# A hybrid decoder layer on one core: conv gates applied behind the next weight's low part, four MLP operands fetched at another place, and the MLP's first weight sum tied behind the last residual

## The chip, the cores and the metric

The kernel runs on one core of a Trainium2 chip. The metric is the device time of one execution in microseconds (us). Three executions of the kernel before took 2448.47, 2448.91 and 2451.01 us, a median of 2448.91. TensorE (PE) multiplies, VectorE (DVE) and ScalarE (ACT) do element-wise work, GpSimd (POOL) and SyncE (SP) here mostly issue DMA transfers: SP loads weights from the inputs, POOL moves intermediate results to and from DRAM.

## What is computed

One layer over 512 tokens of width 2048, all in float32, cut to what matters here:

```python
h = rmsnorm(x, g_mix[l])
z = jnp.einsum('bsd,dc->bsc', h, w_in[l])
cb, cc, cv, q, k, v, f_logit, gate_c, gate_a = jnp.split(z, SPLIT_POINTS, axis=-1)
conv_y = cb * causal_dwconv(cc * cv, conv_w[l])
conv_branch = jnp.einsum('bsc,cd->bsd', conv_y, w_conv_out[l])
attn = forgetting_attention(q, k, v, log_f)
attn_branch = jnp.einsum('bsc,cd->bsd', attn, w_attn_out[l])
gc = jax.nn.sigmoid(gate_c + b_gate[l, :D_MODEL])
ga = jax.nn.sigmoid(gate_a + b_gate[l, D_MODEL:])
merged = gc * conv_branch + ga * attn_branch
x = x + jnp.einsum('bsd,de->bse', merged, w_mix_out[l])
h = rmsnorm(x, g_mlp[l])
u = jnp.square(jax.nn.relu(jnp.einsum('bsd,df->bsf', h, w_ff1[l])))
x = x + jnp.einsum('bsf,fd->bsd', u, w_ff2[l])
```

## The kernel before

**High and low parts.** PE multiplies operands of a short float format. Each float32 operand is therefore split into a high part, a rounded copy that ACT makes (`th`, L103), and a low part, what is left, which DVE makes by subtraction (`tl`, L104). A product takes three matmuls: high by high, high by low, low by high. A weight's low part is needed by the third matmul of its chunk (`gemm_t`, L424 to L426) or by the last third of a quarter's matmuls (`mm_rows` and `mm_cols`, L146 to L175).

**attn_out, column groups 0 to 3.** `attn_out(c)` multiplies the attention result by 512 columns of w_attn_out, in two chunks of 4 x 128 rows (`wchunk`: SP loads `raw`, then the split). Each chunk is 48 matmuls of 128x512. When a group is done, `cons_at(j)` runs for its four blocks j on DVE: `merged`, which holds the conv branch, is multiplied by the conv gate (`hg`, loaded by POOL), and the attention result times its own gate (`gt`, loaded by SP, L1006) is added (L975 or L979, through `onto`). Groups 0 and 3 have had their conv gates multiplied in earlier; groups 1 and 2 do it here. The `hg` tiles share two buffers, by the parity of j, so `hg` 2 can be loaded only when the multiplication by `hg` 0 is over. Between the chunks of group c, `all_of(c - 1)` makes the seven sums of the merged blocks that the next product needs (`M`, split as above), and `bring` fetches the held conv branch of the group two further on from `held_d` (L994).

**Products by seven.** w_mix_out, w_ff1 and w_ff2 are multiplied by a Strassen-like scheme: the weight's block of columns is cut into quarters X[0,0], X[0,1], X[1,0], X[1,1] (SP, L208), and seven products A11, A12, S1, S2, S3, S4, A22 are made of quarters or sums of quarters (L113) and of the matching operands on the other side. `Group.head` does A11 and A12, `tail2` or `tail3` the other five. After each product a list of steps (`after`) runs.

**From w_mix_out to w_ff1.** `Mix` takes the four column groups g of w_mix_out: `put` adds the residual `xr` (L116) and writes `x1_d` (L1092); `turn` transposes the result on PE, and ACT and DVE scale it and, in the last group, split it straight into the operands `A11` and `A12` of w_ff1 (L1113, L1114) or keep it in `F` (L1117). `first_of` and `sums` form the operands S1, S3, S2, S4, A22; in groups 0 to 2 `give` writes their high and low parts to `h_d` (L1133). In group 3 `begin_part` makes a tile for each w_ff1 operand and has POOL fetch what was written before: from `f_d` for A11 and A12 (L1068), from `h_d` for the other five (L1066). The last groups' share is written in directly by `Mix.out`. The first group of w_ff1, `g0`, loads X[0,0], X[1,0], X[0,1] and X[1,1] on SP and computes A11, A12, then S1, S3, S2, S4, A22; its first weight sum is X[0,1] - X[0,0] (`first_sum`, L113), which S1 multiplies, and its third is X[1,1] - X[0,1], which S3 multiplies.

**Order.** A scheduler orders each engine's instructions by priorities that follow from the program's order; an instruction in `tc.keep_in_program_order` keeps its place there against the others so marked, and `tc.issue_after(i)` puts instructions behind i. Each engine then executes its own queue in order, and a waiting instruction holds up all that is behind it on its engine; so do SP and POOL with the DMA transfers that they issue.

Of the kernel before, what the change touches and what calls it, by code (L numbers as in the profile page):

```python
# [8 lines left out]
F32 = mybir.dt.float32  # L9
# [3 lines left out]
ALU = mybir.AluOpType  # L13
# [5 lines left out]
KT = D // P  # L19
# [26 lines left out]
def tile_hybrid_block(ctx: ExitStack, tc, x, g_mix, w_in, b_f, b_gate, conv_w, w_conv_out,  # L46
                      w_attn_out, w_mix_out, g_mlp, w_ff1, w_ff2, g_final, out):
    nc = tc.nc
    x, out = x[0], out[0]
# [13 lines left out]
    def bank(i, name):  # L63
        return psum.tile([P, S], F32, tag=f"p{i}", name=name)

    def pair(i, dt, name):

        return main.tile([P, 2, D], dt, tag=f"t{i}", name=name)

    def otile(shape, name, dt=F32):  # L70
        return main.tile(shape, dt, tag="o", name=name, bufs=5)
# [9 lines left out]
    h_d = dram.tile([P, 5, 2, KT // 2 - 2, HS], F32, name="h_d")  # L81
# [20 lines left out]
    def split(src, hi, lo, one=1.0):  # L102
        a = nc.scalar.activation(out=hi, in_=src, func=AF.Copy, scale=one)  # L103
        b = nc.vector.tensor_tensor(out=lo, in0=src, in1=hi.bitcast(F32), op=ALU.subtract)  # L104
        return a, b

    def split_in_order(*how):

        for i in split(*how):
            tc.keep_in_program_order(i)  # L110

    def sub(out, a, b):
        return nc.vector.tensor_tensor(out=out, in0=a, in1=b, op=ALU.subtract)  # L113

    def add(out, a, b):
        nc.vector.tensor_tensor(out=out, in0=a, in1=b, op=ALU.add)  # L116

    def parts(shape, at=0):

        q, w = shape[1:]  # L120
        return tuple(main.tile([P, WBUF], F32R, tag=tag, name=tag, bufs=2)[:, at:at + q * w]
                     .rearrange("p (q c) -> p q c", q=q) for tag in ("th", "tl"))
# [67 lines left out]
    class Group:  # L190
# [128 lines left out]
            self.plus(s2, d)  # L319
            self.put(1, 0, s2)  # L320

        def first_sum(self):

            self.pinned = True
            X = self.X
            X[0, 1] = self.load(0, 1)
            tc.keep_in_program_order(sub(X[0, 0], X[0, 1], X[0, 0]))

        def tail2(self):

# [69 lines left out]
    def wchunk(view, k0, c0, slot):  # L400

        raw = main.tile([P, 4, S], F32, tag=f"x{slot}", name="raw")
        nc.sync.dma_start(out=raw, in_=view[k0 * P:(k0 + 4) * P, c0:c0 + S].rearrange("(q p) c -> p q c", p=P))
        hi, lo = parts([P, 4, S])
        split(raw, hi, lo)
        return hi, lo

    turns, cycle = [0], [0, 3, 2]

    def slot():  # L410
# [49 lines left out]
    class Quarters:  # L460
# [20 lines left out]
        def put(self, n, src, ts=slice(0, HS), one=1.0):  # L481
            split(src[:, :, ts], self.ST[n][:, 0, :, ts], self.ST[n][:, 1, :, ts], one)
# [326 lines left out]
    n = 0  # L809
# [162 lines left out]
    def onto(c, j, g, op):  # L972
        if c in whole_of:
            o = whole_of[c][:, :, j % 2, j // 2, :]
            nc.vector.tensor_tensor(out=o, in0=o, in1=g.rearrange("p (h s) -> p h s", h=2), op=op)  # L975
        else:
            for h in range(2):
                o = merged[c][h][:, j % 2, j // 2, :]
                nc.vector.tensor_tensor(out=o, in0=o, in1=g[:, h * HS:(h + 1) * HS], op=op)  # L979
# [17 lines left out]
    def attn_out(c, banks, last=False, **how):  # L997

        def cons_at(j, ps):
            if c not in GATED:  # L1000
                hg = pm.tile([P, S], F32, tag=("xr", "s1")[j % 2], name="hg")
                nc.gpsimd.dma_start(out=hg, in_=g_d[0, 4 * c + j])
                onto(c, j, hg, ALU.mult)
            g = otile([P, S], "gt")
            nc.sync.dma_start(out=g, in_=g_d[1, 4 * c + j])
            nc.vector.tensor_tensor(out=g, in0=ps, in1=g, op=ALU.mult)  # L1006
            onto(c, j, g, ALU.add)
            if last and j == 2:
                M.place(3, [(n, 3) for n in ("A11", "A12", "S1", "S2")])
                M.place(2, [("S4", 3), ("S3", 3), ("A22", 3), ("A22", 2)])  # L1010
                for e in range(2):
                    nc.gpsimd.dma_start(out=M.at["A22", 2][e].bitcast(F32), in_=m22[e].bitcast(F32))
                quads3.update(M.quads(3, merged[3]))
                quads3["A11"]()
            if last and j == 3:
                quads3["A12"]()

        gemm_t(w_attn_out, CT, c * S, aact, banks, cons_at, **how)
# [31 lines left out]
    n = turns[0] + 1  # L1050
# [4 lines left out]
    Q2 = {}  # L1055
# [4 lines left out]
    SPLIT = ("S1", "S3", "S2", "S4", "A22")  # L1060

    def begin_part(n, k):

        Q2[n] = pair(k, F32R, n).rearrange("p e (q s) -> p e q s", q=KT // 2)
        if n in SPLIT:
            nc.gpsimd.dma_start(out=Q2[n][:, :, :KT // 2 - 2].bitcast(F32), in_=h_d[:, SPLIT.index(n)])  # L1066
        else:
            nc.gpsimd.dma_start(out=Q2[n][:, 1, :KT // 2 - 2].bitcast(F32), in_=f_d[:, int(n == "A12")])  # L1068

    def split_part(n):  # L1070
        lo = Q2[n][:, 1, :KT // 2 - 2]
        split_in_order(lo.bitcast(F32), Q2[n][:, 0, :KT // 2 - 2], lo)

    class Mix:
# [13 lines left out]
        def put(self, i, j, v):  # L1088
            g = self.g
            c = g * S + j * HS  # L1090
            add(v, v, self.x.pop((i, j)))
            nc.gpsimd.dma_start(out=x1_d[2 * i:2 * i + 2, :, c:c + HS].rearrange("t p c -> p t c"), in_=v)  # L1092
            waiting.append(lambda: self.turn(i, j, v))
            if (i, j) == (0, 0):
                self.rows(1, 1, otile([P, 2, HS], "xr"))
                self.rows(0, 1, pm.tile([P, 2, HS], F32, tag="xr", name="xr"))
# [83 lines left out]
    for g in range(4):  # L1180
        mix = mixes[g] = Mix(g)
        after = Steps()
        if g == 0:
            for n, n2 in zip(("A11", "A12", "S1", "S3", "S2"), ("S1", "S3", "S2", "S4", "A22")):
                after.add(n, quads3[n2])
        if g == 3:
            after.add("S1", mix.fourth, lambda: begin_part("A12", 4))
        late = g == 1
        for n in ("A12", "S3") if late else ("A11", "S1"):
            after.add(n, turn_waiting)  # L1190
        after.add("A22", turn_first)
        if before:
            after.add("A12" if late else "A11", before.first_of, before.sums)
            for n, part in (("A12", "S1"), ("S1", "S3"), ("S2", "A22")):
                after.add(n, lambda before=before, part=part: before.give(part))
        if g < 3:
            after.add("S2", mix.fourth)
        else:
            after.add("A12", lambda: begin_part("A11", 0))
            after.add("S2", lambda: begin_part("S1", 1), lambda: begin_part("S3", 3))  # L1200
            after.add("S4", lambda: split_part("A11"))
            after.add("S3", lambda: begin_part("S2", 5))
            after.add("A22", lambda: begin_part("S4", 6), lambda: begin_part("A22", 2), lambda: split_part("A12"))
        group = groups[g]
        group.after = after
        if g == 0:
            after.add("A11", group.first_sum)
        if g == 3:
            group.mid["A22"] = turn_first
        group.head(True, between=groups[1].first if g == 0 else lambda: None)  # L1210
        (group.tail2 if g < 3 else group.tail3)()
        before = mix
    def factors(common, r):

        ms = const.tile([P, NT], F32, name="ms")
        nc.vector.tensor_reduce(out=ms, in_=ss2, axis=AX.X, op=ALU.add)
        nc.gpsimd.tensor_tensor(out=r, in0=ms, in1=mhalf.to_broadcast([P, NT]), op=ALU.pow)
        ones = const.tile([P, P], F32, name="ones")
        nc.vector.memset(ones, 1.0 / S)
        pt = bank(6, "mean")  # L1220
        nc.tensor.matmul(pt[:, :NT], ones, ms, start=True, stop=True)
        mean, back = (const.tile([P, 1], F32, name=n) for n in ("mean", "back"))
        nc.vector.tensor_reduce(out=mean, in_=pt[:, :NT], axis=AX.X, op=ALU.add)
        nc.gpsimd.tensor_tensor(out=common, in0=mean, in1=mhalf, op=ALU.pow)
        nc.vector.reciprocal(out=back, in_=common)
        nc.vector.tensor_scalar(out=r, in0=r, scalar1=back, scalar2=None, op0=ALU.mult)
        nc.vector.tensor_tensor(out=r, in0=r, in1=r, op=ALU.mult)
# [49 lines left out]
    def ff1(g, banks):  # L1277
# [3 lines left out]
    common, turned = const.tile([P, 1], F32, name="common"), const.tile([P, NT], F32, name="turned")  # L1281

    g0 = ff1(0, ((5,), (0,), (1,), (7,)))
    g0.after = Steps(A11=[g0.first_sum, turn_waiting, mix.first_of],
                     A12=[lambda: mix.out("S1", mix.s1), mix.sums, lambda: factors(common, turned)])
    g0.head(True)
    for n in SPLIT[1:]:
# [248 lines left out]
```

## Time and profile before

| | us |
|---|---|
| median of three executions | 2448.91 |
| profiled execution, its own time | 2452.95 |
| its span in the profile | 2451.2 |
| PE busy | 2410.0 |
| DVE busy | 2042.6 |
| ACT busy | 1203.0 |
| POOL busy | 280.0 |

The profile shows one execution. In a timeline row stand the start in us from the span's beginning, the duration, the engine, the line of the kernel, the operation, the tile written and the tiles read, and in brackets the idle time of the engine before the instruction with what ended it. Some starts overlap the end of the row before, because the instructions of an engine are pipelined; a chain's length is therefore read from start to start. Rows of stretches give for each engine the busy time, then PE's granted clock (1.00 is full), the share of the DMA engines that was busy and the bytes moved. In the queue rows stand packets, MB and the time that the packets took as a share of 16 engines.

### The profile page before, as it was taken

The page shows a single profiled execution, that of the slowest core. Times are in us where ns is not written, and L with a number is a line of the kernel's source. Part 1 is how long each engine was busy: PE and PEld are TensorE (multiplying, and loading weights), DVE is VectorE, ACT ScalarE, POOL GpSimd, SP SyncE. Part 2 cuts the span into 40 slices and gives each one's busy share as a digit, 9 for nine tenths or more (in the row PEclk, how much of TensorE's full clock was granted, in tenths as well). Part 3 has the DMA queues.
Part 4 walks back from the last instruction along what each step waited for, and adds up shares of the span by engine and source line. Part 5 has one row for each costly group of instructions (what it writes and reads, how often), then busy time and mean ns, then how long its engine had stood idle before and what let it go on. Part 6 is the DMA issues. An engine that isn't in the chain of part 4 may idle for free.

```text
span 2451.2 us, 41539 instructions
## 1 busy us (share of the span) xinstructions
PE 2410.0 (98%) x17800; PEld 2266.2 (92%) x17800; DVE 2042.6 (83%) x1725; ACT 1203.0 (49%) x1233; POOL 280.0 (11%) x450
## 2 busy tenths in 40 slices
PE   8999999999999999999999999999999999999998
PEld 8999899999999999899899999999997888888886
DVE  6987777788888778898889898898978888889898
ACT  6443433345455444355656666666655333333334
POOL 0100000111121111112300000000011001100000
PEclk9999999999999999999999999999999999999999
DMA  7564444444656655757855655656587576655663
GB/s 250 181 187 147 154 135 143 142 154 167 216 170 214 213 189 189 237 162 252 306 183 186 228 189 199 236 182 228 194 304 271 168 248 227 236 190 183 245 223 103
DMA packets 287628, 491.97 MB, mean 201 GB/s; under 512 B 11900, under 2 KB 199412, under 8 KB 287060
## 3 DMA queue, kind: packets, MB, share of 16 engines
q1 hardware_dynamic: 237072, 283.20, 36.3%
q0 software_dynamic: 49504, 205.02, 22.5%
q8 instruction: 139, 2.28, 0.4%
q10 hardware_dynamic: 868, 1.10, 0.1%
q14 instruction: 45, 0.37, 0.0%
HBM read 378.65 MB, written 110.10 MB: 199 GB/s over the span
## 4 chain that ended last, share of the span: by engine, by line
PE 86%; DVE 5%; issue 4%; DMA 3%; POOL 1%; ACT 1%; DVEq 0%; SPq 0%; POOLq 0%; ACTq 0%
PE a L157 6%; PE a L153 6%; PE a L155 6%; PE a L175 5%; PE a L173 5%; PE a L172 5%; PE d L157 5%; PE d L153 5%; PE d L155 5%; PE c L153 4%; PE c L155 4%; PE c L157 4%; PE d L175 3%; PE d L173 3%; PE d L172 3%
## 5 line engine op out<-in xcount | busy, mean ns | idle before, releaser
L103 ACT ACTIVATE th<-x 128x2048 fp32r<-128x2048 f32 (+1 forms) x280 | 536.9, 1918 | 501.1 <-DVE x L113 169.3
L104 DVE TENSOR_TENSOR tl<-x,th 128x2048 fp32r<-128x2048 f32 (+1 forms) x280 | 639.5, 2289 | 166.3 <-ACT th L103 151.3
L113 DVE TENSOR_TENSOR x<-x,x 128x2048 f32<-128x2048 f32 (+1 forms) x160 | 366.3, 2289 | 28.5 <-DMA x<-in_w_in_dram 17.4
L103 ACT ACTIVATE th<-y 128x2048 fp32r<-128x2048 f32 (+1 forms) x109 | 185.4, 1702 | 273.8 <-PE a L173 138.8
L104 DVE TENSOR_TENSOR tl<-y,th 128x2048 fp32r<-128x2048 f32 (+1 forms) x109 | 219.1, 2014 | 29.1 <-ACT th L103 28.6
L172 PE MATMUL a<-th,us 128*128 128x512 f32 x512 | 199.4, 389 | 2.2 <-ACT th L103 2.2
L173 PE MATMUL a<-th,us 128*128 128x512 f32 x512 | 199.5, 390 | 0.0
L153 PE MATMUL c<-S,th 128*128 128x256 f32 x848 | 196.7, 278 | 0.0
L155 PE MATMUL c<-S,th 128*128 128x256 f32 x848 | 196.3, 277 | 0.0
L153 PE MATMUL a<-S,th 128*128 128x256 f32 x784 | 182.3, 278 | 0.0
L155 PE MATMUL a<-S,th 128*128 128x256 f32 x784 | 180.9, 277 | 0.0
L153 PEld LDWEIGHTS c<-S,th 128*128 128x128 f32 x848 | 159.4, 188 | 0.3
L155 PEld LDWEIGHTS c<-S,th 128*128 128x128 f32 x848 | 159.4, 188 | 0.0
L155 PEld LDWEIGHTS a<-S,th 128*128 128x128 f32 x784 | 147.4, 188 | 0.0
L153 PEld LDWEIGHTS a<-S,th 128*128 128x128 f32 x784 | 147.3, 188 | 0.0
L175 PE MATMUL a<-tl,us 128*128 128x512 f32 x512 | 137.0, 390 | 0.6 <-DVE tl L104 0.6
L155 PE MATMUL a<-A,th 128*128 128x256 f32 x544 | 126.0, 278 | 2.2 <-DVE A L1114 2.2
L153 PE MATMUL d<-S,th 128*128 128x256 f32 x544 | 128.0, 280 | 0.0
L155 PE MATMUL b<-A,th 128*128 128x256 f32 x544 | 126.4, 278 | 1.3 <-DVE A L104 1.3
L155 PE MATMUL d<-S,th 128*128 128x256 f32 x544 | 127.4, 279 | 0.0
L153 PE MATMUL b<-A,th 128*128 128x256 f32 x544 | 126.4, 278 | 0.0
L153 PE MATMUL a<-A,th 128*128 128x256 f32 x544 | 126.1, 278 | 0.0
(378 smaller groups left out, 6076.5 us busy)
## 6 DMA issues: line engine op xcount, KB each, us to landing
x<-in_w_in_dram SPq DMA_DIRECT2D x86, 1024.0 KB, 5.9
x<-in_w_ff_dram SPq DMA_DIRECT2D x64, 1024.0 KB, 8.5
y<-in_w_ff_dram SPq DMA_DIRECT2D x64, 1024.0 KB, 7.9
us<-s_d POOLq DMA_DIRECT2D x48, 1024.0 KB, 9.5
s_d<-rh POOLq DMA_DIRECT2D x32, 896.0 KB, 5.5
s_d<-r POOLq DMA_DIRECT2D x32, 896.0 KB, 5.9
x<-in_w_mix_out_dram SPq DMA_DIRECT2D x17, 1024.0 KB, 6.9
g_d<-o POOLq DMA_DIRECT2D x32, 256.0 KB, 2.8
```

Source lines behind the costliest of these rows:

```text
L103: a = nc.scalar.activation(out=hi, in_=src, func=AF.Copy, scale=one)
L104: b = nc.vector.tensor_tensor(out=lo, in0=src, in1=hi.bitcast(F32), op=ALU.subtract)
L113: return nc.vector.tensor_tensor(out=out, in0=a, in1=b, op=ALU.subtract)
L153: nc.tensor.matmul(o, hi[:, q, js], Sh, start=first and q == 0 and j == 0, stop=False, skip_group_check=True)
L155: nc.tensor.matmul(o, hi[:, q, js], Sl, start=False, stop=False, skip_group_check=True)
L157: nc.tensor.matmul(o, lo[:, q, js], Sh, start=False, stop=q == nq - 1, skip_group_check=True)
L172: nc.tensor.matmul(o, Sh, hi[:, q, :], start=begin and q == 0, stop=False, skip_group_check=True)
L173: nc.tensor.matmul(o, Sl, hi[:, q, :], start=False, stop=False, skip_group_check=True)
L175: nc.tensor.matmul(o, Sh, lo[:, q, :], start=False, stop=q == nq - 1, skip_group_check=True)
```

## The change

The conv gate multiplications of groups 1 and 2 are put behind the latest low part that `wchunk` has made. `first_sum` of g0 is no longer kept in program order, and is put behind the last residual sum of the last group (`mix.added`), after the steps that turn what is waiting. The fetches of S2, S4 and A22 come in a step of g0's A11, that of S3 after S3 in group 3 of w_mix_out instead of after S2, and the fetches from `h_d` keep their program order. `Mix.put` makes its sum by the same instruction as before, with its handle kept.

```diff
-        def first_sum(self):
+        def first_sum(self, pinned=True):
...
-            tc.keep_in_program_order(sub(X[0, 0], X[0, 1], X[0, 0]))
+            one = sub(X[0, 0], X[0, 1], X[0, 0])
+            if pinned:
+                tc.keep_in_program_order(one)
...
-        split(raw, hi, lo)
+        chunk_low.append(split(raw, hi, lo)[1])
         return hi, lo
+    chunk_low = []
...
                 nc.gpsimd.dma_start(out=hg, in_=g_d[0, 4 * c + j])
-                onto(c, j, hg, ALU.mult)
+                with tc.issue_after(chunk_low[-1].ins):
+                    onto(c, j, hg, ALU.mult)
...
         if n in SPLIT:
-            nc.gpsimd.dma_start(out=Q2[n][:, :, :KT // 2 - 2].bitcast(F32), in_=h_d[:, SPLIT.index(n)])
+            tc.keep_in_program_order(
+                nc.gpsimd.dma_start(out=Q2[n][:, :, :KT // 2 - 2].bitcast(F32), in_=h_d[:, SPLIT.index(n)]))
...
-            add(v, v, self.x.pop((i, j)))
+            self.added = nc.vector.tensor_tensor(out=v, in0=v, in1=self.x.pop((i, j)), op=ALU.add)
...
             after.add("A12", lambda: begin_part("A11", 0))
-            after.add("S2", lambda: begin_part("S1", 1), lambda: begin_part("S3", 3))
+            after.add("S2", lambda: begin_part("S1", 1))
             after.add("S4", lambda: split_part("A11"))
-            after.add("S3", lambda: begin_part("S2", 5))
-            after.add("A22", lambda: begin_part("S4", 6), lambda: begin_part("A22", 2), lambda: split_part("A12"))
+            after.add("S3", lambda: begin_part("S3", 3))
+            after.add("A22", lambda: split_part("A12"))
...
+    def begin_rest():
+        for n, k in (("S2", 5), ("S4", 6), ("A22", 2)):
+            begin_part(n, k)
+
+    def first_sum_after(ins):
+        with tc.issue_after(ins.ins):
+            g0.first_sum(pinned=False)
...
-    g0.after = Steps(A11=[g0.first_sum, turn_waiting, mix.first_of],
+    g0.after = Steps(A11=[turn_waiting, begin_rest, lambda: first_sum_after(mix.added), mix.first_of],
```

## The prediction

> **What bounds the kernel now.** I began with the page's header and busy row.
>
> ```profile
> span 2451.2 us, 41539 instructions
> PE 2410.0 (98%) x17800; PEld 2266.2 (92%) x17800; DVE 2042.6 (83%) x1725; ACT 1203.0 (49%) x1233; POOL 280.0 (11%) x450
> ```
>
> TensorE (PE) is busy 2410.0 of 2451.2 us, so the change matters only where it shortens, lengthens or makes a stall of PE, or alters PE's clock. PE's timeline, which prints the idle time before an instruction and its releaser, shows the stalls in the two places that the diff touches. The first row is the start of attn_out's second chunk of column group 2 (I call the chunks c2k0, c2k4, c3k0, c3k4); its third matmul, the first to read the low part tl, is the second row.
>
> ```profile
> 1000.57 0.39 PE L424 MATMUL pt<-act,th 128*128 128x512 f32 x1
> 1002.96 0.50 PE L426 MATMUL pt<-act,tl 128*128 128x512 f32 x1 [1.78 <-DVE tl L104]
> ...
> 1015.60 0.39 PE L426 MATMUL pt<-act,tl 128*128 128x512 f32 x1
> ...
> 1211.25 0.39 PE L155 MATMUL a<-A,th 128*128 128x256 f32 x1 [2.15 <-DVE A L1114]
> 1217.40 0.38 PE L155 MATMUL b<-A,th 128*128 128x256 f32 x1 [1.30 <-DVE A L104]
> 1230.95 0.36 PE L146 MATMUL d<-S,th 128*128 128x192 f32 x1 [2.06 <-ACT th L103]
> ```
>
> Four stalls, 1.78 + 2.15 + 1.30 + 2.06 = 7.29 us. Cutting the span into stretches shows that they cost more than their own length.
>
> ```profile
> 1000.00:1004.00 4.00, 2.22 (x10) 1.55 (x9) 4.00 (x5) 1.15 (x2) 0.14 (x1) 0.97 0.26 90
> 1004.00:1008.00 4.00, 4.00 (x12) 3.13 (x12) 4.00 (x8) 2.14 (x4) 0.58 (x1) 0.60 0.90 208
> ...
> 1212.00:1216.00 4.00, 4.00 (x21) 3.80 (x20) 3.52 (x4) 3.48 (x10) 2.16 (x3) 0.58 1.01 402
> ...
> 1224.00:1236.00 12.00, 9.94 (x72) 9.73 (x71) 9.89 (x13) 4.26 (x5) 0.56 (x1) 0.86 0.29 116
> ```
>
> The columns are PE, PEld, DVE, ACT and POOL busy, then the granted clock, the share of the DMA engines and GB/s. Behind the 1.78 us stall the clock is 0.60: lost are 4 x 0.03 + 4 x 0.40 = 1.7 us. Behind the stalls of 2.15 and 2.06 it is 0.58 and 0.86 (4 x 0.42 = 1.7 and 12 x 0.14 = 1.7 us); the 1.30 us one is followed by none of its own. I call this a half-clock window, and put its threshold between 1.30 and 1.78 us.
>
> [...]
>
> **The change, part one: the conv gates of column group 2.** The four multiplications by hg move behind the low part of c2k4. In DVE's rows two of them stand ahead of that low part today:
>
> ```profile
> 997.03 0.69 DVE L975 TENSOR_TENSOR merged<-merged,hg 128x512 f32<-128x512 f32 x1 [0.42 <-DMA hg<-g_d]
> 997.64 0.68 DVE L104 TENSOR_TENSOR M<-merged,M 128x512 fp32r<-128x512 f32 x1
> 998.61 0.69 DVE L975 TENSOR_TENSOR merged<-merged,hg 128x512 f32<-128x512 f32 x1 [0.29 <-DMA hg<-g_d]
> 999.22 0.69 DVE L1006 TENSOR_TENSOR gt<-pt,gt 128x512 f32<-128x512 f32 x1
> ...
> 1000.62 2.28 DVE L104 TENSOR_TENSOR tl<-raw,th 128x2048 fp32r<-128x2048 f32 x1
> ...
> 1008.24 0.69 DVE L975 TENSOR_TENSOR merged<-merged,hg 128x512 f32<-128x512 f32 x1
> ...
> 1010.23 2.29 DVE L104 TENSOR_TENSOR tl<-raw,th 128x2048 fp32r<-128x2048 f32 x1
> ```
>
> They take 0.42 + 0.61 + 0.29 + 0.61 = 1.93 us (starts to starts). Comparing the built orders, the sum s now stands ahead of tl too, another 0.6, and the M low part still has to wait some 0.4 for its high part on ACT. So tl starts 1.93 - 0.6 - 0.4 = 0.9 us sooner. PE's third matmul is due two pitches of 0.22 after 1000.57, at 1001.0, and came at 1002.96; the wait goes from 1.9 to 1.0 us. At 1.0 the half-clock window goes too. Won: 0.9 + 1.7 = 2.6 us.
>
> What is late next is the low part of c3k0. In the built order DVE does hg 0, 1 and 2 ahead of it, hg 3 after it. hg 0 and hg 2 share one buffer, so POOL can fetch hg 2 only when multiplication 0 is done. Today's first hg of the later pair starts 1008.24 - 1000.62 = 7.6 us behind c2k4's tl; with tl at 999.7 and s taken out of the stretch that is 999.7 + 7.6 - 0.6 = 1006.7 for multiplication 0, and its end at 1007.4 releases the fetch, at about 1007.5. What a fetch costs there has two near rows: the same hg loads at 994 to 1000 and the merged loads that POOL issues from 1007.42, min/median/max to landing:
>
> ```profile
> DMA to landing us min/median/max: 2.8/2.9/3.1
> ```
>
> ```profile
> L994 POOL DMA_DIRECT2D merged<-held_d x4: 712/723/729, 1007.4 to 1011.5; - x4
> ...
> DMA to landing us min/median/max: 4.9/5.9/6.0
> ```
>
> The first four flew while DVE had PE fed and the DMA engines had gaps; the second at a DMA share of 0.90 (the 1004 to 1008 row). Two of the merged loads now stand right ahead of hg 2 in POOL's queue, so I take 5.0, nearer to 5.9. hg 2 lands at 1012.5, its multiplication (0.6) and tl (2.2) end at 1015.3. PE wants it at 1015.60 - 2.6 = 1013.0: a new stall of 2.3 us, and, above the threshold, a half-clock window of 1.7. Part one: -2.6 + 4.0 = +1.4 us. With 2.9 it is landing 1010.4, end 1013.2, stall 0.2: -2.4. With 5.9: stall 3.2 and 1.7: +2.3. The four gt loads move ahead of the next w_mix load on SP; that load's data is first read behind both chunks of group 3, 96 matmuls or 21 us, so I count nothing. If c3k4's tl, with under 1 us to spare, is late as well, this is inside the upper end.
>
> **Part two: the last residual and the first weight sum of ff1.** DVE's queue today:
>
> ```profile
> 1208.51 2.29 DVE L113 TENSOR_TENSOR x<-x,x 128x2048 f32<-128x2048 f32 x1 [6.33 <-DMA x<-in_w_ff_dram]
> 1210.72 0.48 DVE L1114 SCALAR_TENSOR_TENSOR A<-ptr,cols,A 128x256 fp32r<-128x256 f32 x1
> ...
> 1212.84 2.28 DVE L104 TENSOR_TENSOR tl<-x,th 128x2048 fp32r<-128x2048 f32 x1
> 1215.59 1.76 DVE L104 TENSOR_TENSOR A<-A 128x1536 fp32r<-128x1536 f32 x1 [0.48 <-ACT A L103]
> 1217.79 2.29 DVE L104 TENSOR_TENSOR tl<-x,th 128x2048 fp32r<-128x2048 f32 x1 [0.44 <-ACT th L103]
> ...
> 1226.61 2.29 DVE L113 TENSOR_TENSOR x<-x,x 128x2048 f32<-128x2048 f32 x1
> ...
> 1228.99 1.91 ACT L103 ACTIVATE th<-x 128x2048 fp32r<-128x2048 f32 x1 [2.44 <-DVE one L1432]
> ```
>
> The sub at 1208.51 waits 6.33 us for quarter (0,1) of w_ff1, and two L1114 and two L116 queue behind it, 1210.72 to 1212.84 = 2.12 us. They now run in that idle time. The PE wait at 1211.25 for L1114 goes, though PE then only comes sooner to A12, whose third matmul waits for A's low part (1215.59), which still stands behind the sub. Five S1 matmuls moved ahead of that third matmul wait for the same sub through th, no later than A's low part ends. From sub to the third sum (1226.61) the chain loses 2.12, the waits 0.48 and 0.44 (ACT is no longer held up by L1114), and the reciprocal and turned pair, about 0.29, which now follow it: 3.33 us. If (0,1) lands as today, A12 goes on at 1217.40 - 2.12 - 0.48 = 1214.8, and S3, which waits for th of the third sum, starts at 1230.95 - 3.33 = 1227.6. Part two would be -3.3.
>
> **Part three: what POOL fetches when.** It decides whether (0,1) lands as today.
>
> ```profile
> 1195.12 0.71 POOL L1066 DMA_DIRECT2D S<-h_d  x1 [9.57 <-DMA h_d<-s]
> 1195.83 0.57 POOL L1133 DMA_DIRECT2D h_d<-staged  x1
> ...
> 1208.01 0.71 POOL L1066 DMA_DIRECT2D S<-h_d  x1 [10.01 <-DMA h_d<-f]
> ```
>
> POOL sits 9.57 us in front of the S1 load with four h_d writes behind it, then 10.01 us in front of S3. In the built order the four writes come ahead of S1, the x1_d writes between S1 and S3; S2, S4 and A22 behind both. So the queue has no such pauses, and S3's 1.5 MB go out some 5 to 9 us sooner. What a pause is worth to SP's weight loads shows in the queues' bytes from 1193.5 to 1198.5 and from 1198.5 to 1208.5 (q1 is SP's, q0 POOL's):
>
> ```profile
> q1 hardware_dynamic: 1636, 1.66, 102.0%
> q0 software_dynamic: 31, 0.13, 6.3%
> ```
>
> ```profile
> q0 software_dynamic: 592, 2.62, 65.0%
> q1 hardware_dynamic: 1214, 1.21, 35.3%
> ```
>
> Alone SP's queue moves 1.66 / 5 = 0.33 MB per us, beside POOL's 1.21 / 10 = 0.12. If the whole pause fills with writes, SP is 5 x (0.33 - 0.12) = 1.06 MB behind at 1198.5. Paid back at 0.33 that delays (0,1) by 3.2 us, at 0.12 by 8.7; if POOL's data still start as late as today, by 0. I take 3.2, as POOL must still wait for its own writes before S1 and S3 and for the last residual before S2, and in each such gap SP has the engines. Then part two and three together are 3.2 - 3.33 = -0.1 us (0: -3.3; 8.7: +5.4). PE is not the limit there: A12 goes on at 1214.8 + 3.2 = 1218.0 and has as much work to S3 as today (1217.40 to 1230.95 less the stall of 2.06 is 11.5), done at 1229.5 against S3's 1230.8. I leave both half-clock windows of this stretch as they are, since PE still idles for long before A12's third matmul; the one at S3 is open (a stall of 1.3), which is worth 1.7 down.
>
> [...]
>
> **Sum.** Profiled execution 2452.95 us (span 2451.2, 1.75 outside) + 1.4 - 0.1 = 2454.2. The profiled execution lies 4.04 above the median 2448.91; I take the same off: 2450.2 us.
>
> **Rivals.** (a) Both loads come in time: hg 2 lands in 2.9 and (0,1) as today. For it: the hg rows, and the waits of POOL for its own writes. Against it: a DMA share of 0.9 and 1.0 in both places. 2452.95 - 2.4 - 3.3 - 4.04 = 2443.2. (b) Slower: SP's queue starves. POOL's writes, S1, S3 and then S2, S4, A22 follow each other without a pause, (0,1) lands 8.7 late, and DVE, with tl of A12, A's low part and all of S1 and S3 behind the sub, stands still. From a delay of 3.3 it costs more than part two wins. With hg 2 at 5.9: 2452.95 + 2.3 + 5.4 - 4.04 = 2456.6. For it: both transfers share 16 busy engines. Against it: total bytes do not grow, and the x1_d write of the last residual holds S2 back. (c) hg 2 lands fast, the sub late by 3.2: 2452.95 - 2.4 - 0.1 - 4.04 = 2446.4. Its counterpart, hg 2 late and (0,1) in time, gives 2447.0, by 1.4 - 3.3.
>
> **How the numbers follow.** About 0.2%, 4.9 us, is what a measurement of this kernel can tell from no change: faster is below 2444.0, slower above 2453.8. The forecast, gains given back at hg 2 and at (0,1), has 0.33, (a) 0.25, (b) 0.29, (c) with its counterpart 0.13. (a) ends faster, at 2443.2; a lost window at S3 in (c) adds 0.02: faster 0.27. (b) is slower, mostly, and the forecast's tail of a longer hg wait reaches there: slower 0.30. The rest, 0.43, is within the bound. The range goes from just under (a) to 2456.0, which takes in the smaller delays of (b), and leaves out about 0.2. The likeliest case alone is 2447 to 2453.
>
> **What would show it.** Right: the stall at c2k4 is near 1.0 without a slow clock behind it; a new one at c3k0's tl, with DVE waiting for hg. The L1114 row sits ahead of the sub, and the sub's releaser is still the w_ff1 load, some 3 us later than 1208.5; POOL's S3 load goes out before 1204; S3's first matmul is within 1.5 us of 1230.95, reckoned from the same start. Wrong: hg is never waited for; or the sub starts by 1209 or after 1214; or the third sum waits for (1,1); or a wait past 1240.

## The result, and the profile after

Over 20 executions of each on the same chips the changed kernel took 2455.88 us (2451.27 to 2462.66) and the kernel before 2450.60 us (2447.39 to 2454.15). The ratio is 1.0022, 95% interval 1.0016 to 1.0028: slower by 5.4 us, 3.9 to 6.9. The prediction was 2450.2 us in a range from just under 2443.2 to 2456.0, with "within 0.2%" as the likeliest. The time is inside the range, 0.1 us from its upper end; the change of 0.22% is just past the bound on the slow side, and its interval (0.16 to 0.28%) reaches to both sides of that bound.

The profiled execution of the changed kernel took 2454.11 us (span 2452.4), 1.8 us under its median, while the one of before, 2452.95, lies 2.4 over the median of its 20. The difference of the two profiles, 1.2 us, is therefore less than the change costs; they show where time goes, and the sizes are taken from the experiments. Header and busy row of the page after:

```profile
span 2452.4 us, 41546 instructions
## 1 busy us (share of the span) xinstructions
PE 2407.9 (98%) x17800; PEld 2263.3 (92%) x17800; DVE 2042.3 (83%) x1725; ACT 1203.3 (49%) x1233; POOL 281.6 (11%) x450
```

PE's work is the same, so the place to look is its stalls. PE's timeline after, the rows with idle time that answer to those of before, and the new ones (the line numbers have moved by 3 to 6):

```profile
1002.52 0.50 PE L429 MATMUL pt<-act,tl 128*128 128x512 f32 x1 [1.23 <-DVE tl L104]
1014.80 0.50 PE L429 MATMUL pt<-act,tl 128*128 128x512 f32 x1 [1.11 <-DVE tl L104]
...
1061.63 0.95 PE L175 MATMUL d<-tl,M 128*128 128x256 f32 x6 [0.52 <-DVE tl L104]
1068.49 0.97 PE L175 MATMUL a<-tl,M 128*128 128x256 f32 x6 [0.94 <-DVE tl L104]
...
1216.02 0.36 PE L146 MATMUL b<-A,th 128*128 128x192 f32 x1 [3.63 <-ACT A L103]
1218.74 0.58 PE L153 MATMUL c<-S,th 128*128 128x256 f32 x1 [2.23 <-ACT th L103]
1220.61 0.58 PE L155 MATMUL b<-A,th 128*128 128x256 f32 x1 [0.43 <-DVE A L104]
1234.22 0.36 PE L146 MATMUL d<-S,th 128*128 128x192 f32 x1 [1.36 <-ACT th L103]
1240.88 0.39 PE L153 MATMUL a<-S,th 128*128 128x256 f32 x1 [0.81 <-ACT th L103]
```

At c2k4 the stall is shorter, 1.23 instead of 1.78 us. For that there are three others: at c3k0 (1014.80), and two at the first quarters of w_mix_out (1061.63 and 1068.49), where PE did not wait before. At the MLP the stalls of 2.15, 1.30 and 2.06 us have become 3.63, 2.23, 0.43, 1.36 and 0.81. Just ahead of that, near 1180 us, the changed kernel waits less: 0.35 us in all against 0.94 and 0.85 before. The clock, from the cut into stretches:

```profile
1000.00:1004.00 4.00, 2.77 (x12) 1.99 (x11) 4.00 (x5) 0.93 (x2) 0.00 (x0) 1.00 0.37 95
1004.00:1008.00 4.00, 4.00 (x19) 3.33 (x18) 4.00 (x8) 2.55 (x4) 1.44 (x2) 1.00 0.95 252
...
1216.00:1224.00 8.00, 5.32 (x24) 4.83 (x25) 8.00 (x8) 4.91 (x10) 3.01 (x1) 0.57 1.02 414
1224.00:1236.00 12.00, 10.64 (x92) 10.43 (x91) 9.65 (x16) 5.30 (x7) 0.56 (x1) 1.00 0.21 84
```

The half-clock window behind c2k4 is gone (1.00 instead of 0.60 from 1004 to 1008), and so is the one behind S3. At the MLP one long stretch at 0.57 has taken the place of the two, and costs as much as they did together: 8 x 0.43 = 3.4 us.

DVE's timeline after tells what the new stalls wait for:

```profile
1008.41 0.68 DVE L978 TENSOR_TENSOR merged<-merged,hg 128x512 f32<-128x512 f32 x1
1011.86 0.69 DVE L978 TENSOR_TENSOR merged<-merged,hg 128x512 f32<-128x512 f32 x1 [2.77 <-DMA hg<-g_d]
1012.47 2.28 DVE L104 TENSOR_TENSOR tl<-raw,th 128x2048 fp32r<-128x2048 f32 x1
...
1206.83 0.69 DVE L1096 TENSOR_TENSOR o<-o,xr 128x512 f32<-128x512 f32 x1
1214.40 2.29 DVE L113 TENSOR_TENSOR x<-x,x 128x2048 f32<-128x2048 f32 x1 [6.88 <-DMA x<-in_w_ff_dram]
1216.61 2.28 DVE L104 TENSOR_TENSOR tl<-x,th 128x2048 fp32r<-128x2048 f32 x1
1218.81 1.75 DVE L104 TENSOR_TENSOR A<-A 128x1536 fp32r<-128x1536 f32 x1
```

DVE waits 2.77 us for hg 2 right ahead of c3k0's low part, and the first weight sum of ff1 starts at 1214.40 instead of 1208.51, still for want of quarter (0,1).

ACT's timeline after shows that quarter (1,0), which the prediction did not reckon with, lands late too:

```profile
1210.44 1.92 ACT L103 ACTIVATE th<-x 128x2048 fp32r<-128x2048 f32 x1 [5.57 <-DMA x<-in_w_ff_dram]
...
1214.48 1.49 ACT L103 ACTIVATE A<-A 128x1536 fp32r<-128x1536 f32 x1
```

ACT waits 5.57 us for (1,0), and so makes A's high part late, for which PE waits 3.63 us. PE then has only half a us of work until its next stall, at 1218.74, which the first weight sum's high part ends. So it is the late (0,1) that ends PE's waiting. (In e7 below, where (1,0) came sooner, the first of these stalls is 0.79 us and the second 4.46.)

POOL's and SP's bytes from 1204.5 to 1209.5, ahead of that landing, are in the queue rows after:

```profile
q0 software_dynamic: 324, 1.72, 84.2%
q1 hardware_dynamic: 322, 0.33, 18.6%
```

Columns are packets, MB and the share of the engines. In that stretch of before POOL's queue ran nearly dry: it moved 0.77 MB, of which 0.09 after 1207.0, and SP's moved 0.81.

```profile
q1 hardware_dynamic: 803, 0.81, 45.5%
q0 software_dynamic: 240, 0.77, 42.2%
```

### The profile page after: what moved, and what is told of

It is laid out like the page before. It is cut to its first block, busy times and chain, and to the rows that moved or that the text cites. A ratio compares the mean times of both kernels' runs of the same rounds, so it can differ in the third digit from the quotient of the medians.

```text
span 2452.4 us, 41546 instructions
## 1 busy us (share of the span) xinstructions
PE 2407.9 (98%) x17800; PEld 2263.3 (92%) x17800; DVE 2042.3 (83%) x1725; ACT 1203.3 (49%) x1233; POOL 281.6 (11%) x450
## 4 chain that ended last, share of the span: by engine, by line
PE 83%; DVE 7%; issue 4%; DMA 4%; ACT 1%; POOL 1%; SPq 0%; DVEq 0%; POOLq 0%; ACTq 0%
PE a L157 6%; PE a L153 6%; PE a L155 6%; PE a L175 5%; PE a L173 5%; PE a L172 5%; PE d L153 5%; PE d L155 5%; PE d L157 5%; PE c L153 4%; PE c L155 4%; PE c L157 4%; DVE tl L104 3%; PE d L175 3%; PE d L173 3%
```

## The experiments

The theory was: (A) the fetch of hg 2 costs PE twice, at once and again where DVE's lateness surfaces; (C) the sum behind the residual wins, and POOL's new order takes more than that back, because the weight quarters land late. The main rivals: all of the loss lies at the MLP, the moved waits cost nothing, or the transfers are hidden. Each kernel was timed 11 or 12 times, against 29 or 33 executions of the kernel before on the same chip. The us are the ratio less one, times 2451.

| kernel | ratio to before | 95% interval | us |
|---|---|---|---|
| changed kernel | 1.0022 | 1.0016 to 1.0028 | +5.4 |
| e1 part one | 1.0005 | 0.9997 to 1.0014 | +1.2 |
| e2 part one, own buffers | 0.9999 | 0.9991 to 1.0008 | -0.2 |
| e3 part two | 0.9989 | 0.9980 to 0.9998 | -2.7 |
| e4 part three | 1.0022 | 1.0013 to 1.0031 | +5.4 |
| e5 parts one and two | 0.9997 | 0.9988 to 1.0006 | -0.7 |
| e6 e2 and part two | 0.9983 | 0.9974 to 0.9992 | -4.2 |
| e7 changed, own buffers | 1.0007 | 0.9998 to 1.0016 | +1.7 |
| e8 parts two and three, S3 late | 0.9985 | 0.9976 to 0.9994 | -3.7 |
| e9 changed, S3 late | 0.9995 | 0.9987 to 1.0004 | -1.2 |
| e10 part three, S3 late | 1.0004 | 0.9996 to 1.0012 | +1.0 |
| e11 e6 and e8 together | 0.9984 | 0.9976 to 0.9993 | -3.9 |

**e1: part one alone.**

```diff
-        split(raw, hi, lo)
+        chunk_low.append(split(raw, hi, lo)[1])
...
-                onto(c, j, hg, ALU.mult)
+                with tc.issue_after(chunk_low[-1].ins):
+                    onto(c, j, hg, ALU.mult)
```

> Part one alone: the conv gates of group 2 behind the low part of c2k4; first sum and fetches as before. Theory A (the fetch of hg 2 costs twice): DVE waits 2 to 3 us for hg 2, PE stalls some 1.5 us at the third matmul of c3k0, and DVE, which has no idle time from there to the first quarters of w_mix_out, stays about 2 us late, so that PE stalls again there (0.8 and 1.2 us in the changed kernel, none before). Net of the 0.5 us won at c2k4: slower than before by 2 to 4 us, and nothing different from before after 1180 us but a shift. Rival B (all of the loss lies at the MLP): within 1 us of before, or faster by the 0.5 us and a half-clock window of 1.7.

The time does not tell +1.2 from nothing (-0.7 to +3.4), and the 2 to 4 us expected are at most partly there. The trace does show the expected wait and stalls. DVE's and PE's timelines of e1:

```profile
1011.65 0.69 DVE L976 TENSOR_TENSOR merged<-merged,hg 128x512 f32<-128x512 f32 x1 [3.14 <-DMA hg<-g_d]
```

```profile
1061.44 0.97 PE L175 MATMUL d<-tl,M 128*128 128x256 f32 x6 [0.48 <-DVE tl L104]
1068.29 0.97 PE L175 MATMUL a<-tl,M 128*128 128x256 f32 x6 [0.93 <-DVE tl L104]
```

The same wait and the same two late stalls as in the changed kernel, without its parts two and three. The wait and the first of the stalls belong to part one; whether the second does, e2 and e3 tell.

**e2: as e1, with other buffers for hg 2 and 3 of group 2.**

```diff
-                hg = pm.tile([P, S], F32, tag=("xr", "s1")[j % 2], name="hg")
+                hg = pm.tile([P, S], F32, tag=("xr", "s1")[j % 2], name="hg") if j < 2 or c == 1 else otile([P, S], "hg")
```

> As e1, but hg 2 and 3 of group 2 get buffers of the pool of gt tiles, so that their fetch no longer waits for the multiplications by hg 0 and 1. Theory A: DVE no longer waits for hg 2, the stall at c3k0 and the two at w_mix_out vanish, the shorter stall at c2k4 stays: 2 to 4 us under e1, 0.5 to 2 us under before. If the wait is not the cause (rival: four multiplications in front of c3k0's low part are too many by themselves, 4 x 0.6 = 2.4 us), the stalls at w_mix_out stay, and e2 lies within 1 us of e1.

DVE's timeline of e2 at the same place:

```profile
1007.70 0.68 DVE L104 TENSOR_TENSOR M<-merged,M 128x512 fp32r<-128x512 f32 x1
1008.30 1.88 DVE L976 TENSOR_TENSOR merged<-merged,hg 128x512 f32<-128x512 f32 x3
1010.11 2.28 DVE L104 TENSOR_TENSOR tl<-raw,th 128x2048 fp32r<-128x2048 f32 x1
```

The multiplications by hg follow each other and the low part starts 2.4 us sooner than in the changed kernel (1010.11 against 1012.47). The stall at c3k0 and the first of the two at w_mix_out are gone. The second is not. PE's timelines of e2 and then of e3, whose gates are those of before:

```profile
1065.66 0.97 PE L175 MATMUL a<-tl,M 128*128 128x256 f32 x6 [0.89 <-DVE tl L104]
```

```profile
1066.71 0.96 PE L175 MATMUL a<-tl,M 128*128 128x256 f32 x6 [0.46 <-DVE tl L104]
```

So theory A is wrong on this stall: 0.89 us stay without the wait for hg 2, against 0.93 with it, and half of it is there without part one. Against e1 the gain is only 1.4 us where 2 to 4 were expected, and within the intervals; three pairs with and without these buffers (e2 and e1, e6 and e5, e7 and the changed kernel) give 1.4, 3.5 and 3.7 us, and together they show that the wait costs time.

**e3: part two alone** (`first_sum_after(mix.added)` behind `turn_waiting`; POOL's order is that of before).

```diff
-    g0.after = Steps(A11=[g0.first_sum, turn_waiting, mix.first_of],
+    g0.after = Steps(A11=[turn_waiting, lambda: first_sum_after(mix.added), mix.first_of],
```

> Part two alone: the first weight sum of ff1 behind the last residual; gates and fetches as before. Theory C: quarter (0,1) lands as before, the sub starts at about 1208.5 us, and the two L1114 and two residual sums run in the wait ahead of it. S3's first matmul starts some 3 us sooner than 1230.95; faster than before by 2 to 3.5 us. Rival D (PE's wait is only moved): the longer single wait before A12's third matmul costs as much as the two it replaces, same as before within 1 us.

DVE's and PE's timelines of e3:

```profile
1205.02 0.48 DVE L1116 SCALAR_TENSOR_TENSOR A<-ptr,cols,A 128x256 fp32r<-128x256 f32 x1 [0.54 <-ACT A L1115]
...
1209.06 2.29 DVE L113 TENSOR_TENSOR x<-x,x 128x2048 f32<-128x2048 f32 x1 [1.42 <-DMA x<-in_w_ff_dram]
```

```profile
1213.81 0.39 PE L153 MATMUL c<-S,th 128*128 128x256 f32 x1 [1.06 <-ACT th L103]
1215.28 0.39 PE L155 MATMUL b<-A,th 128*128 128x256 f32 x1 [0.61 <-DVE A L104]
...
1228.29 0.35 PE L146 MATMUL d<-S,th 128*128 128x192 f32 x1 [2.10 <-ACT th L103]
```

The sub waits for the load as before, but the four instructions that it held up have run. S3 starts 2.7 us sooner. That speaks against rival D, that the wait is only moved, and so does the time, -2.7 us (-4.9 to -0.5), though the end of its interval touches that rival's 1 us. In this execution no half-clock window followed any of these stalls (the clock is 1.00 from 1208 to 1240), where before shows two.

**e4: part three alone.**

```diff
-            nc.gpsimd.dma_start(out=Q2[n][:, :, :KT // 2 - 2].bitcast(F32), in_=h_d[:, SPLIT.index(n)])
+            tc.keep_in_program_order(
+                nc.gpsimd.dma_start(out=Q2[n][:, :, :KT // 2 - 2].bitcast(F32), in_=h_d[:, SPLIT.index(n)]))
...
-            after.add("S2", lambda: begin_part("S1", 1), lambda: begin_part("S3", 3))
+            after.add("S2", lambda: begin_part("S1", 1))
...
-            after.add("S3", lambda: begin_part("S2", 5))
+            after.add("S3", lambda: begin_part("S3", 3))
...
-    g0.after = Steps(A11=[g0.first_sum, turn_waiting, mix.first_of],
+    g0.after = Steps(A11=[g0.first_sum, turn_waiting, begin_rest, mix.first_of],
```

> Part three alone: POOL's fetch order; gates and first sum as before. Theory C: POOL's writes and the S3 fetch now move beside SP's weight loads, quarter (1,0) lands some 10 us and (0,1) 4 to 6 us later than before, the L1114 behind the sub are late by as much, and PE with them: slower than before by 4 to 6 us. Rival D (bytes are the same, the transfers are hidden): the sub starts within 1 us of 1208.5 and the time is that of before within 1 us.

It costs as much as the whole change. DVE's timeline of e4, and PE's:

```profile
1211.96 2.29 DVE L113 TENSOR_TENSOR x<-x,x 128x2048 f32<-128x2048 f32 x1 [10.30 <-DMA x<-in_w_ff_dram]
```

```profile
1214.70 0.58 PE L155 MATMUL a<-A,th 128*128 128x256 f32 x1 [5.93 <-DVE A L1115]
```

The wait of 6.33 us for quarter (0,1) has grown to 10.30, and the stall that was 2.15 us to 5.93. That the transfers are hidden is ruled out.

**e5 and e6: parts one and two, and the same with e2's buffers.**

> The change without its part three: gates and first sum as changed, POOL's fetches and writes as before. Theory C (part three is the whole loss): e1 and e3 add, +1 and -3 us: 1 to 3 us faster than before and 6 to 8 us faster than the changed kernel; quarter (0,1) lands within 1.5 us of 1209. Rival (the first sum behind the residual costs when hg makes DVE late): not faster than before.

> e2 and e3 together: gates with buffers of their own, first sum behind the last residual, fetches as before. Theory A and C: no wait for hg, sub at about 1209; the fastest so far, 3 to 5 us under before and 1 to 2 us under e5. If hg's wait costs nothing in the end, e6 equals e5.

e5 lies 6.1 us under the changed kernel by the ratios, as expected; the 1 to 3 us under before are not shown (-0.7, -2.9 to +1.5). In its trace the sub starts at 1207.53. e6 is 4.2 us under before (2.0 to 6.4), as expected, and beats both kernels; it lies 3.5 us under e5, more than the 1 to 2 expected.

**e7: the changed kernel with e2's buffers, nothing else.**

> The changed kernel with buffers of their own for hg 2 and 3 and nothing else altered. Theory A: the wait for hg and the three stalls behind it vanish, the late weight quarters stay: 1 to 3 us faster than the changed kernel, still slower than before by 2 to 4 us. Rival B: same as the changed kernel.

+1.7 instead of +5.4: the two intervals meet only at their edges, at 1.0016. By the ratios the fetch of hg 2 costs the changed kernel 3.7 us, more than the 1 to 3 expected and more than e1 shows for it; from the two intervals I estimate 1 to 6. The traces show less: from c2k4's third matmul to SP's first load of w_ff1 the changed kernel takes 181.7 us (1002.52 to 1184.24) and e7 180.1 (1001.90 to 1181.95), 1.7 us apart. The stall at w_mix_out that Theory A expected to vanish with the others, the second, stands here too, with 0.91 us.

**e8: parts two and three with the S3 fetch late.**

```diff
-            after.add("S3", lambda: begin_part("S3", 3))
...
-        for n, k in (("S2", 5), ("S4", 6), ("A22", 2)):
+        for n, k in (("S3", 3), ("S2", 5), ("S4", 6), ("A22", 2)):
```

> Parts two and three without the gates, and with the S3 fetch put behind the last x1_d write, next to S2, S4 and A22; the four h_d writes stay ahead of the S1 fetch. Theory E (the 1.5 MB of S3 beside the weight quarters are what delays them): quarter (0,1) lands within 1.5 us of 1209, and the time is within 1 us of e3, some 3 us under before. Rival F (the writes in POOL's former pause are it): (0,1) lands at 1212 or later as in the changed kernel, and the time is 2 to 6 us over before.

POOL's timeline, DVE's and ACT's of e8:

```profile
1193.16 1.14 POOL L1136 DMA_DIRECT2D h_d<-f  x2 [0.72 <-DVE f L104]
1196.02 0.72 POOL L1069 DMA_DIRECT2D S<-h_d  x1 [1.71 <-DMA h_d<-s]
...
1210.88 2.15 POOL L1069 DMA_DIRECT2D S<-h_d  x3 [1.62 <-PE a L155]
```

```profile
1210.30 2.29 DVE L113 TENSOR_TENSOR x<-x,x 128x2048 f32<-128x2048 f32 x1 [2.06 <-DMA x<-in_w_ff_dram]
```

```profile
1207.67 1.92 ACT L103 ACTIVATE th<-x 128x2048 fp32r<-128x2048 f32 x1 [2.10 <-DMA x<-in_w_ff_dram]
```

The four writes still go ahead of the S1 fetch, and ACT now waits for quarter (1,0) until 1207.67. But the sub starts at 1210.30, not 1214.40, or 25.4 us instead of 30.2 behind SP's first load of w_ff1 (1184.86 and 1184.24), and the loss has become a gain of 3.7 us. So it is the early S3 fetch that makes (0,1) late in a way that costs; what the writes cost, e10 tells. With S3 late the scheduler also puts the third sum's low part ahead of the turned pair, which may be a part of the gain.

**e9 to e11.** e9 is the changed kernel with e8's edit, e10 part three with it, e11 e6 and e8 together.

> The changed kernel with one fetch moved: S3 behind the last x1_d write, ahead of S2 (which also lets the scheduler put the third sum's low part ahead of the turned pair). Theory E: quarter (0,1) lands 3 to 5 us sooner than in the changed kernel, counted from the issue of (0,0); 4 to 7 us faster than the changed kernel, within 1.5 us of e5. Rival F (the writes ahead of S1): same as the changed kernel within 1 us.

> Part three alone with S3 behind the last x1_d write; gates and first sum as before. Tells what the four writes ahead of S1 cost by themselves, as (1,0) is late and (0,1) is not. Theory E: (1,0) lands near 1208 as in e4 and e8 but PE does not wait for it; same as before within 1.5 us, 4 to 6 us under e4. Rival F: the late (1,0) holds up th of A12 and with it A's low part, 3 us or more over before.

> e6 and e8 together: buffers of their own for hg 2 and 3, first sum behind the last residual, the writes ahead of S1, S3 behind the last x1_d write. If the causes named are all there is, as fast as e6 and e8, 3 to 5 us under before; the order of the four writes gives nothing more.

e9: one fetch moved lets the sub start 25.5 us behind SP's first load of w_ff1 (1186.69 to 1212.19) instead of 30.2. It takes 6.6 us off the changed kernel, and the time is then that of e5, within the intervals. e10: the writes ahead of S1, with S3 late, cost 1.0 us, which the measurement does not tell from nothing, and 4.4 us less than e4. e11 is as fast as e6, so the order of the writes and of S3 gives nothing further. The order of the four writes was not tried alone with S3 early.

## Why the prediction came out as it did

The point was that the gains are given back at two new waits, at hg 2 and at quarter (0,1). Both are where it said. The time came out 5.7 us above the forecast: 1.7 of it is the base (below), and some 4 the balance of gains and losses, forecast +1.3 and measured +5.4. That the time lies in the range is owed to the width that was taken for rival (b), and it is a matter of 0.1 us.

Of the signs that the prediction named, these came: the shorter stall at c2k4 without a slow clock, the new one at c3k0 with DVE waiting for hg, the L1114 pair (now L1119, at 1203.87 and 1204.90) ahead of the sub, the sub still waiting for the w_ff1 load, the S3 fetch before 1204 (at 1199.92). Two did not, and both are of part three. The sub, due some 3 us later than 1208.5, started at 1214.40, past the 1214 that was named as a sign of being wrong (1213.6 with the 0.8 us taken off by which the whole program was late there). S3's first matmul, due within 1.5 us of 1230.95, came at 1234.22, 2.5 us late with the same 0.8 taken off.

- **Part one, won at c2k4:** forecast 0.9 us and a half-clock window, 1.7. The low part did come 0.9 us sooner, counted from DVE's wait for hg just ahead (992.51 to 1000.62 before, 992.99 to 1000.18 after); as that wait itself ended 0.48 later, the stall fell by 0.55 only (1.78 to 1.23). The window went in this execution, but a part of its 1.7 us seems to come back: of the five kernels with the gates of before, the two with a slow clock behind c2k4 (before, e8) do not wait at 1066 us, and the three without (e3, e4, e10) wait 0.46, 0.50 and 0.46 there.
- **Part one, the wait for hg 2:** forecast landing at 1012.5 after 5.0 us; the multiplication started at 1011.86, as the fetch went ahead at 1008.2 and took 3.7. The stall at c3k0 was 1.11 us, not 2.3, and no half-clock window followed (the granted clock was 1.00 from 1012 to 1020). What the forecast missed is the second payment: DVE makes up little between 1012 and 1060. It starts c3k0's low part 2.24 us later than before (1012.47 against 1010.23) and is still 1.95 late at a low part of w_mix_out (1059.29 against 1057.34), and PE stalls there for 0.52 us. The 0.94 us at 1068.49 are not a part of it, as e2 and e7 show. The stalls come to 1.6 us; e7 puts the whole at 3.7 us. That this is near the 4.0 forecast is luck, as the terms are others; the distance from 1.6 to 3.7 is within the uncertainty, and what else there is to it stays open.
- **Part two:** forecast -3.3, measured -2.7 (e3, -4.9 to -0.5); S3 started 2.7 us sooner, and the sub at 1209.06. The size is right; that both half-clock windows of this stretch would stay was not so in e3's execution.
- **Part three:** this is the term that was mis-sized. I took 3.2 us from bounds of 0 and 8.7, arguing that POOL's own waits would leave SP gaps. e4 measured 5.4 us (3.2 to 7.6), and the changed kernel less e5 gives 6.1; in the changed kernel the sub started 5.9 us late, 0.8 of it because the whole program was that far behind (SP issued the first of these loads at 1184.24 instead of 1183.46). The gaps were not there while S3's 1.5 MB moved: from 1204.5 to 1209.5 SP's queue sent 322 packets with 0.33 MB and POOL's 324 with 1.72 MB, and SP's 0.33 / 5 = 0.07 MB per us is less than the 0.12 that I had read as the rate beside POOL. That mean was of two unlike halves: SP's queue moved 0.41 MB beside POOL's 1.56 from 1198.5 to 1203.5, 0.08 MB per us, and 0.80 beside 1.06 in the next 5 us.
- **Rival (b)**, SP's queue starved, is what happened in kind, but the delay was 5.1 us and not 8.7 (5.9 less the 0.8). It names "S3 and then S2, S4, A22 without a pause"; e8 shows that S3 decides. S2, S4 and A22 went out too late to matter for (0,1): in the changed kernel they were issued from 1210.36 on, and from 1209.5 to 1214.5 POOL's queue moved 0.47 MB and SP's 1.41. Rival (a) fell with both its terms.
- **The base.** I took 4.04 us off for the profiled execution, from three runs. By 20 runs it lay 2.4 above the median, which moves the forecast 1.7 us up.

## What to carry to other kernels

A wait put off can be paid again where its engine has not caught up: look at the next 50 us of the engine that waits, not only at the next instruction. But a later stall is not the wait's because it comes behind it: look for it in a kernel without the wait. Before a bulk fetch is moved forward, list which weight loads of another queue are under way in that stretch, and read what both queues move there: in the changed kernel SP's queue, with packets of 1 KB in the mean (0.33 MB in 322), got 0.33 of 2.05 MB from 1204.5 to 1209.5 beside POOL's with 5 KB (1.72 MB in 324). And a buffer that two steps share ties the later fetch to the earlier use, so that moving the use moves the fetch too.

## What was not expected of the hardware

In these traces a stall of PE was not always followed by a half-clock window. Behind c2k4, e3 and e8 both show 1.82 us of idle time; the stretches from 1004 to 1008 are, for e3 and then for e8:

```profile
1004.00:1008.00 4.00, 4.00 (x18) 3.27 (x19) 4.00 (x8) 1.81 (x3) 0.00 (x0) 1.00 0.60 155
```

```profile
1004.00:1008.00 4.00, 3.51 (x10) 2.81 (x11) 4.00 (x8) 1.26 (x2) 0.00 (x0) 0.69 0.50 129
```

The granted clock was 1.00 in the one and 0.69 in the other. At S3 it is the same: a slow clock followed the stalls of 2.06 us (before, 0.57 from 1232 to 1236) and 2.41 us (e5, 0.62 from 1228 to 1232), and none those of 2.04, 2.10 and 2.38 us (e2, e3, e6). So the threshold that the prediction put between 1.30 and 1.78 us, an estimate from the one trace of before, did not hold: at 1.82 to 2.41 us the window came in some of these executions and not in others, and its 1.7 us belongs into the sum with a chance, not as a term. Why it falls one way or the other was not tried.
